# A hybrid four-layer kernel: the third layer's 16-token region gathered into one tile, and a forget gate whose scan adds two terms

## The chip, the cores and the metric

The kernel runs on one core of a Trainium2 chip. Its engines are TensorE (PE for products, PEld for the weight loads beside them), VectorE (DVE), ScalarE (ACT), GpSimd (POOL) and SyncE (SP), which issues the DMAs. Each engine works through its own queue in order and waits on semaphores for the others. The metric is the device time of one execution in microseconds, as the median of several runs. All of it runs in one launch.

## The reference

A meta prefix of 16 tokens and 1024 tokens of width 1024 pass four layers, each a residual branch behind an RMS norm: sliding-window attention, an mLSTM, an HGRN2 (the third layer, which the change touches), and attention again. The third layer has 8 heads with 128 key and 128 value channels:

```python
def hgrn2_chunkwise(q, k, v, log_f):
    ...
    def step(S, inp):
        q_, k_, v_, lf = inp
        A = jnp.cumsum(lf, axis=2)
        o_inter = jnp.einsum('bhtd,bhde->bhte', q_ * jnp.exp(A), S)
        dec = jnp.where(causal[..., None], A[:, :, :, None, :] - A[:, :, None, :, :], -jnp.inf)
        att = jnp.einsum('bhtd,bhtsd,bhsd->bhts', q_, jnp.exp(dec), k_)
        o = o_inter + jnp.einsum('bhts,bhse->bhte', att, v_)
        A_last = A[:, :, -1]
        S_new = jnp.exp(A_last)[..., None] * S + jnp.einsum('bhsd,bhse->bhde', k_ * jnp.exp(A_last[:, :, None] - A), v_)
        return S_new, o
...
    lb = lower_bound.astype(jnp.float32)
    lf = jnp.logaddexp(jnp.log(lb), jnp.log1p(-lb) + jax.nn.log_sigmoid(fpre.astype(jnp.float32)))
    kk = -jnp.expm1(lf)
```

The decay between two tokens differs by channel, so the attention matrix isn't one product: `exp(A_t - A_s)` has to be split at a point between s and t, and the kernel does that by levels of halves.

## The kernel before

Activations lie transposed: 128 channels on the partitions, the 1040 tokens along the row, in chunks of 400, 384 and 256. Each projection (`proj`, the products at L231) splits weight and activation into a high and a low part and sums three products. Weights arrive by DMA in halves of 128x512, which ACT casts and DVE subtracts (`split`, L195 and L196).

In the third layer (`layer_c`) every head has a forget gate `f_proj` (L1188 to L1202: log-sigmoid of z, the logaddexp with the lower bound, a scan by block of 128 tokens which gives A, and N, the log of the key less A), a query projection `q_proj` (L1211 is its last DVE step) and a mixer. The gate's `lna` and `lnb` are the logs of the two parts of the bound, `dif` is their difference, and each is a column of a tile named `lb` in the profile.

The mixer works on five regions: the first holds the 16 meta tokens, the other four two blocks of 128 tokens each. For a region, `level` builds a tile X for each of the levels 0 to 7 (levels 3 to 7 in the region of 16): two DVE steps fill the halves with exponents (L1247, L1248), ACT takes Exp (L1249), DVE multiplies the later half by Q (L1250). Level 7 is the diagonal (L1240, L1241). The X tiles rotate over 14 buffers. `levels_mm` then issues the products of all the levels in one burst (L1263 for levels 0 and 1, 32x64 and 32x32; L1273 for the others, 32x32, or 16x16 in the region of 16), into PSUM tiles `pm`. `tail0` masks and adds them on DVE (L1290, L1294, L1300), copies the attention tile together on POOL and ACT (`att`, L1302 to L1306), and prepares the decayed keys and queries (L1309, L1315). `tail1` transposes the keys on PE (`pt`, L1326), ACT copies them (`kT`, L1328), `states` multiplies them with the values (`pa`, L1336) and carries the state S on (L1341, L1343), and `tail2` makes the output (`po`, L1357, L1359).

What sets the order: PE's instructions stand as the program writes them. `weave(a, b)` merges two lists of steps so that both advance by the same share of their summed costs; steps of the list of a region carry a cost of GAP for each level and BURST for the products, and the tails carry lags (TAIL_LAG, KT_LAG, ATT_LAG) that only push the next step back. Each region's list is woven with the tail of the region ahead, and the whole with the projections of the next head, the gates and the output products, which fill PE between bursts. The order on the other engines comes from a scheduler at the build, which works with its own estimates and prefers steps wrapped in `hi`. All PSUM tiles share eight buffers.

## Time and profile before

| what | us |
| --- | --- |
| median of three runs | 2601.44 |
| lowest and highest | 2598.78, 2603.09 |
| profiled execution | 2596.91 |
| its span (first to last instruction) | 2595.1 |

In the rows of the profile, a timeline's row has the start in us from the span's begin, the duration of the merged instructions, engine, line, operation and tiles, and in brackets the idle time ahead of it with what ended it. A row of a group has, behind the bar, the busy time in us, the mean duration of one in ns, and the engine's idle time just ahead. A row of windows has the stretch, its length, the busy time of each engine and the granted TensorE clock. Matmuls are pipelined: their listed durations overlap, so the step from start to start is what one costs.

### The profile page before, as it was taken

The numbers are of one execution on the slowest core, as the hardware profiler recorded it, in microseconds if no ns is written. First come the engines' busy times: TensorE is split into PE (matmuls) and PEld (weight loads), VectorE is DVE, ScalarE is ACT, GpSimd is POOL, SyncE is SP. The second block draws the span as 40 slices with busy tenths as digits, with TensorE's granted clock in tenths as the row PEclk, the third lists the DMA queues.
The fourth block names the chain that finished last, engine by engine and source line by source line (L and its number), as shares of the span: only waits on it lengthen the run. The fifth ranks groups of instructions, "written<-read, shape, count | busy, mean of one in ns | idle before, by whom it ended". The sixth has DMA issues, their size and how long they took to land.

```text
span 2595.1 us, 54389 instructions
## 1 busy us (share of the span) xinstructions
PE 2547.2 (98%) x20446; PEld 2486.5 (96%) x20446; DVE 1960.2 (76%) x5290; ACT 1689.9 (65%) x4434; POOL 245.6 (9%) x564
## 2 busy tenths in 40 slices
PE   8999999999999999999999999999999999999999
PEld 8899999999999999999999999999999999999999
DVE  7897898775656564747474688988888978887996
ACT  8766766666464645555555757877676857767772
POOL 0321231000000000000000000010000000321330
PEclk9999999999999999999999999999999999999999
DMA  5223212021111111111111111111111113212112
GB/s 157 62 66 93 59 43 69 30 67 56 44 54 46 50 49 51 42 58 41 51 46 52 51 34 34 34 35 34 38 39 34 34 51 91 62 44 85 56 42 78
DMA packets 86058, 140.21 MB, mean 54 GB/s; under 512 B 12425, under 2 KB 39186, under 8 KB 85794
## 3 DMA queue, kind: packets, MB, share of 16 engines
q1 hardware_dynamic: 85794, 136.73, 17.1%
q8 instruction: 161, 2.64, 0.4%
q14 instruction: 103, 0.84, 0.1%
HBM read 121.83 MB, written 4.27 MB: 49 GB/s over the span
## 4 chain that ended last, share of the span: by engine, by line
PE 65%; DVE 13%; ACT 9%; issue 2%; DMA 2%; POOL 0%; SPq 0%; DVEq 0%; ACTq 0%; POOLq 0%
PE pj L231 29%; PE pj L326 15%; PE pj L281 10%; DVE wl L196 1%; ACT Sm L737 1%; PE po L1019 1%; PE po L1021 1%; PE pa L1035 1%; DVE Sm L734 1%; PE po L773 1%; ACT wh L195 1%; PE pt L755 1%; ACT X L1249 1%; PE pj L277 1%; DVE t L457 1%
## 5 line engine op out<-in xcount | busy, mean ns | idle before, releaser
L231 PE MATMUL pj<-uh,wh 128*128 128x256 f32 (+2 forms) x2688 | 914.8, 340 | 6.9 <-ACT uh L401 6.4
L231 PE MATMUL pj<-ul,wh 128*128 128x256 f32 (+2 forms) x2688 | 864.2, 322 | 0.3
L231 PE MATMUL pj<-uh,wl 128*128 128x256 f32 (+2 forms) x2688 | 864.3, 322 | 0.0
L231 PEld LDWEIGHTS pj<-uh,wh 128*128 128x128 f32 x2688 | 507.4, 189 | 16.3 <-ACT uh L401 6.4
L231 PEld LDWEIGHTS pj<-ul,wh 128*128 128x128 f32 x2688 | 507.9, 189 | 6.4 <-DVE ul L196 0.9
L231 PEld LDWEIGHTS pj<-uh,wl 128*128 128x128 f32 x2688 | 507.2, 189 | 0.0
L196 DVE TENSOR_TENSOR wl<-wr,wh 128x512 fp32r<-128x512 f32 (+1 forms) x338 | 234.7, 703 | 52.0 <-ACT wh L195 49.3
L195 ACT CAST wh<-wr 128x512 fp32r<-128x512 f32 (+1 forms) x338 | 202.9, 613 | 103.6 <-PE pj L326 32.7
L326 PE MATMUL pj<-yh,wh 128*128 128x384 f32 (+2 forms) x768 | 253.2, 330 | 9.8 <-DVE x L329 8.3
L329 DVE TENSOR_TENSOR x<-x,pj 128x384 f32<-128x384 f32 (+2 forms) x480 | 234.7, 509 | 32.8 <-PE pj L326 31.6
L326 PE MATMUL pj<-yl,wh 128*128 128x384 f32 (+2 forms) x768 | 245.8, 320 | 0.0
L326 PE MATMUL pj<-yh,wl 128*128 128x384 f32 (+2 forms) x768 | 245.8, 320 | 0.0
L281 PE MATMUL pj<-wh,uh 128*128 128x256 f32 (+1 forms) x768 | 232.7, 303 | 0.0
L281 PE MATMUL pj<-wl,uh 128*128 128x256 f32 (+1 forms) x768 | 216.4, 282 | 0.0
L281 PE MATMUL pj<-wh,ul 128*128 128x256 f32 (+1 forms) x768 | 215.9, 281 | 0.0
L737 ACT ACTIVATE Sm<-Sm,s 128x257 f32<-128x257 f32 (+2 forms) x272 | 131.1, 483 | 88.4 <-DVE s L734 85.9
L740 POOL TENSOR_TENSOR Sm<-Sm,s 128x512 f32<-128x512 f32 (+2 forms) x136 | 139.3, 1024 | 403.5 <-DVE s L739 383.3
L458 ACT ACTIVATE t<-t 128x384 f32<-128x384 f32 (+2 forms) x240 | 117.9, 491 | 76.5 <-DVE t L457 75.0
L326 PEld LDWEIGHTS pj<-yh,wh 128*128 128x128 f32 x768 | 144.5, 188 | 14.0 <-DVE x L329 10.4
L195 ACT CAST yh<-r 128x384 fp32r<-128x384 f32 (+2 forms) x120 | 57.0, 479 | 152.0 <-PE pj L326 136.3
L457 DVE SCALAR_TENSOR_TENSOR t<-pj,t 128x400 f32<-128x400 f32 (+2 forms) x168 | 86.5, 515 | 81.6 <-ACT t L456 80.3
L281 PEld LDWEIGHTS pj<-wh,uh 128*128 128x128 f32 x768 | 144.7, 188 | 2.2
(296 smaller groups left out, 5468.3 us busy)
## 6 DMA issues: line engine op xcount, KB each, us to landing
wr<-in_b_win SPq DMA_DIRECT2D x124, 256.0 KB, 2.8
wr<-in_a_win SPq DMA_DIRECT2D x80, 256.0 KB, 2.8
wr<-in_c_win SPq DMA_DIRECT2D x64, 256.0 KB, 2.8
wr<-in_a_wout SPq DMA_DIRECT2D x32, 256.0 KB, 3.0
wr<-in_b_wout SPq DMA_DIRECT2D x32, 256.0 KB, 2.7
t<-t SPq DMA_DIRECT2D x100, 48.0 KB, 1.9
cs<-in_rope SPq DMA_DIRECT2D x11, 400.0 KB, 3.6
cs<-in_rope SPq DMA_DIRECT2D x11, 384.0 KB, 3.5
```

The costliest lines, as they stand in the source:

```text
L195: s.copy(h, src)
L196: v.tensor_tensor(l, src, h.bitcast(F32), op=ALU.subtract)
L231: pe.matmul(acc[:, :cn], a[:, k, :], b[:, k, c0 : c0 + cn], start=(k == 0 and i == 0), stop=(k == KT - 1 and i == 2))
L277: pe.matmul(acc[:48, :nc], um[0][:, k, :], m[:, kk, :], start=(k == 0 and m is wh), stop=(k == KT - 1 and m is wl))
L281: pe.matmul(acc[:cn, :nc], a[:, k, c0 : c0 + cn], m[:, kk, :], start=(k == 0 and j == 0), stop=(k == KT - 1 and j == 2))
L326: pe.matmul(acc[:, :cn], a[:, k, mc], b, start=(k == 0 and i == 0), stop=(k == 1 and i == 2))
L329: v.tensor_tensor(x[:, m, c0 : c0 + cn], x[:, m, c0 : c0 + cn], acc[:, :cn], op=ALU.add)
L457: v.scalar_tensor_tensor(a[:, :cn], z, 0.0, a[:, :cn], op0=ALU.min, op1=ALU.subtract)
L458: s.activation(a[:, :cn], a[:, :cn], AF.Exp)
L734: v.tensor_tensor_reduce(Sm[:nq, u, :nk], S[:nq, u, :nk], R["masks"][:nq, P + mo : P + mo + nk], rq, sinks[u], ALU.add, ALU.min, st[:nq, u ...
L737: s.activation(Sm[:nq, u, : nk + 1], Sm[:nq, u, : nk + 1], AF.Exp, scale=-1.0, bias=st[:nq, u : u + 1], accum_out=den[:nq, u : u + 1])
L740: g.tensor_tensor(Sm[:nq, :, :nk], Sm[:nq, :, :nk], den[:nq].rearrange("p (u c) -> p u c", c=1).to_broadcast([nq, 2, nk]), op=ALU.mult)
```

## The change

Three things change in the third layer.

The forget gate. The logaddexp was built from `max(LS + dif, 0)`, then `+ lna + T1`; now it is `max(LS, -dif) + lnb` in one TENSOR_SCALAR, and the scan adds T1 itself: each step adds the element of `t1` and the element of `ls` to the running sum, where it multiplied by ones and added before. One SCALAR_TENSOR_TENSOR a chunk goes. At the layer's start, one ACT step makes `-dif`.

The region of 16 tokens. `first_levels` writes levels 3 to 7 into slices of one X tile and takes one Exp over its 80 columns. Its products no longer have a burst of their own; they are issued between the levels of region 1's burst, into a PSUM tile of their own, and its `tail0` follows that burst.

The order. Region 0 has no list to weave any more. The tail of the head before is woven with region 1; regions 0 and 1 have their tails one behind the other, woven with region 2; region 1's burst has a cost of 1.1 BURST.

```diff
-            R["lna"], R["lnb"], R["dif"] = lna, lnb, dif
+            s.mul(lna, dif, -1.0)
+            R["ndif"], R["lnb"], R["dif"] = lna, lnb, dif
...
-                v.tensor_scalar(LS, LS, dif, 0.0, op0=ALU.add, op1=ALU.max)
-                v.scalar_tensor_tensor(LS, LS, lna, T1, op0=ALU.add, op1=ALU.add)
+                v.tensor_scalar(LS, LS, ndif, lnb, op0=ALU.max, op1=ALU.add)
                 for b in CHUNK_BLOCKS[n]:
                     q0, nq = blk(b)
-                    v.tensor_tensor_scan(A[:, q0 : q0 + nq], ones[:, :nq], ls[:, q0 - c0 : q0 - c0 + nq],
-                                         0.0, ALU.mult, ALU.add)
+                    qs = slice(q0 - c0, q0 - c0 + nq)
+                    v.tensor_tensor_scan(A[:, q0 : q0 + nq], t1[:, qs], ls[:, qs], 0.0, ALU.add, ALU.add)
...
+            def first_levels():
+                A, NL, Q = (R[z, h][:, :16] for z in ("A", "N", "Q"))
+                X0 = xt()
+                X = {lv: X0[:, 16 * (lv - 3) : 16 * (lv - 2)] for lv in range(3, 8)}
+                for lv in range(3, 7):
+                    Av, Nv, Qv, Xv, mid = halves(lv, A, NL, Q, X[lv])
+                    v.tensor_tensor(Xv[:, :, 0, :], mid, Nv[:, :, 0, :], op=ALU.add)
+                    v.tensor_tensor(Xv[:, :, 1, :], Av[:, :, 1, :], mid, op=ALU.subtract)
+                v.tensor_tensor(X[7], A, NL, op=ALU.add)
+                s.activation(X0[:, :80], X0[:, :80], AF.Exp)
+                for lv in range(3, 7):
+                    Av, Nv, Qv, Xv, mid = halves(lv, A, NL, Q, X[lv])
+                    v.tensor_tensor(Xv[:, :, 1, :], Xv[:, :, 1, :], Qv[:, :, 1, :], op=ALU.mult)
+                for lv in X:
+                    W["X", 0, lv] = X[lv]
...
-            def levels_mm(r, lvs):
-                for lv in lvs:
+            def levels_mm(r):
+                for lv in range(8):
+                    if r == 1 and lv > 2:
+                        level_mm(0, lv)
                     level_mm(r, lv)
...
-                lvs = list(range(8)) if r else [3, 4, 5, 6, 7]
-                st = []
-                for lv in lvs:
+                st = [] if r else [S(0.0, first_levels)]
+                for lv in range(8 if r else 0):
                     st.append(S(0.0, level, r, lv))
                     st.append([GAP, lambda: None, None])
-                st.append(S(BURST if r else 0.2 * BURST, levels_mm, r, lvs))
-                st.append(S(0.0, tail0, r))
+                if r:
+                    st.append(S(BURST if r > 1 else 1.1 * BURST, levels_mm, r))
+                    st += [S(0.0, tail0, z) for z in ((0, 1) if r == 1 else (r,))]
                 main.append(st)
...
-            if h:
-                tails[0].append(held)
+            mx = main[0]
+            for r in range(1, 5):
+                mx += weave(main[r], last)
+                last = [[TAIL_LAG, lambda: None, None]]
+                if r == 1:
+                    last += ([held] if h else []) + tails[0]
+                last += tails[r]
             held = end
-            mx = []
-            for r in range(5):
-                mx += weave(main[r], last)
-                last = [[TAIL_LAG, lambda: None, None]] + tails[r]
             body += weave(mx, fill)
```

The rows below are the instructions as they stand in an engine's queue, with line, operation, tiles (with their numbers) and the shape written.

PE, head 0, the region of 16 tokens before: five products in a burst of their own, between projections (`pj`).

```order
L231 MATMUL pj_19320<-uh,wl_19096 128x256
L1273 MATMUL pm_19351<-X_19315 16x16
L1273 MATMUL pm_19351<-X_19327 16x16
L1273 MATMUL pm_19351<-X_19332 16x16
L1273 MATMUL pm_19351<-X_19337 16x16
L1273 MATMUL pm_19351<-Q_19275,X_19348 16x16
L231 MATMUL pj_19320<-uh,wh_19095 128x256
```

PE, head 0, the same products now, in region 1's burst (L1293 is L1273 moved down), the 16x16 ones between the 32x32 ones.

```order
L1293 MATMUL pm_19394<-X_19345 32x32 x8
L1293 MATMUL pm_19403<-X_19313 16x16
L1293 MATMUL pm_19394<-X_19350 32x32 x8
L1293 MATMUL pm_19403<-X_19313 16x16
L1293 MATMUL pm_19394<-X_19361 32x32 x8
L1293 MATMUL pm_19403<-X_19313 16x16
L1293 MATMUL pm_19394<-X_19366 32x32 x8
L1293 MATMUL pm_19403<-X_19313 16x16
L1293 MATMUL pm_19394<-X_19371 32x32 x8
L1293 MATMUL pm_19403<-Q_19273,X_19313 16x16
L1293 MATMUL pm_19394<-Q_19273,X_19382 32x32 x8
```

The burst now begins six 256-wide products behind the place where the lone one stood, and region 0's transposition, state and output products come behind it.

DVE, head 0, region 3, before: from the two multiplies behind the gate's TENSOR_SCALAR for the second chunk to the last multiply by Q that the burst needs (the last row). The rows of L1200 are the scans.

```order
L1250 TENSOR_TENSOR X_19814<-X_19814,Q_19275 128x32x4
L1250 TENSOR_TENSOR X_19819<-X_19819,Q_19275 128x64x2
L1197 SCALAR_TENSOR_TENSOR t_19702<-t_19702,lb_18765,t_19701 128x384
L1247 TENSOR_TENSOR X_19830<-r_18841,N_18842 128x128
L1200 SCALAR_TENSOR_TENSOR r_19515<-ones,t_19702 128x128 x3
L1240 TENSOR_TENSOR X_19842<-r_18841,N_18842 128x256
L1202 SCALAR_TENSOR_TENSOR r_19516<-r_19516,lb_18766,r_19515 128x384
L1248 TENSOR_TENSOR X_19830<-r_18841 128x128
L1343 SCALAR_TENSOR_TENSOR S_19838<-S_19632,s_19750,pa_19835 128x128
L1191 SCALAR_TENSOR_TENSOR t_19778<-pj_19717,t_19777 128x256
L1343 SCALAR_TENSOR_TENSOR S_19840<-S_19838,s_19750,pa_19835 128x128
L1250 TENSOR_TENSOR X_19830<-X_19830,Q_19275 128x128
```

DVE, the same place now: the gate's TENSOR_SCALAR (L1197), the last two multiplies (L1270, with X_19811 the last that the burst needs), and the scans (L1201) behind them.

```order
L1193 TENSOR_TENSOR r_19552<-t_19691,pj_19582 128x384
L1322 TENSOR_REDUCE rd_19719<-t_19716 128x64
L1197 TENSOR_SCALAR t_19691<-t_19691,lb_18765,lb_18766 128x384
L1270 TENSOR_TENSOR X_19806<-X_19806,Q_19273 128x64x2
L1270 TENSOR_TENSOR X_19811<-X_19811,Q_19273 128x128
L1332 TENSOR_TENSOR X_19930<-X_19930,Q_19273 128x256
L1201 SCALAR_TENSOR_TENSOR r_19551<-t_19690,t_19691 128x128 x3
```

The last multiply moved from behind the gate's scans and the next chunk's first step to ahead of the scans.

ACT, head 0, the copy of region 0's transposed keys (`kT` of 16x128, the last row of each piece) before:

```order
L454 ACTIVATE t_19308<-pj_19283 128x384
L455 ACTIVATE t_19308<-t_19308 128x384
L456 ACTIVATE t_19308<-t_19308,consts 128x384
L1309 ACTIVATE X_19549<-r_18841 128x256
L1315 ACTIVATE X_19552<-N_18842,r_18841 128x128 x2
L458 ACTIVATE t_19308<-t_19308 128x384
L195 CAST wh_19969<-wr_19971 128x512
L1328 COPY kT_19406<-pt_19405 16x128
```

ACT, the same copy now, with region 1's attention copies (L1326, L1328), region 2's Exps (L1269) and two weight casts ahead of it:

```order
L1326 COPY att_18794<-pm_19385 64x2x64
L1328 COPY att_18794<-pm_19385 32x2x32 x2
L1269 ACTIVATE X_19531<-X_19531 128x256
L1269 ACTIVATE X_19526<-X_19526 128x256
L1269 ACTIVATE X_19540<-X_19540 128x256
L454 ACTIVATE t_19455<-pj_19333 128x256
L195 CAST wh_19956<-wr_19958 128x512
L455 ACTIVATE t_19455<-t_19455 128x256
L195 CAST wh_19956<-wr_19962 128x512
L456 ACTIVATE t_19455<-t_19455,consts 128x256
L1269 ACTIVATE X_19569<-X_19569 128x256
L1350 COPY kT_19516<-pt_19515 16x128
```

The copy moved behind region 1's burst and part of region 2's levels; on PE, six projection products now stand between its transposition and the state product, where there were twelve of them, region 1's burst and six more.

More of the change, by code (lines that the diff above doesn't have):

```diff
@@ L1183, in evac @@
                 cs = slice(c0, c0 + cn)
-                lna, lnb, dif = (R[key][:, h : h + 1] for key in ("lna", "lnb", "dif"))
+                ndif, lnb, dif = (R[key][:, h : h + 1] for key in ("ndif", "lnb", "dif"))
                 z = acc[:, :cn]
@@ L1232, in xt, with halves @@
                 return R["mix"].tile([P, 256], F32, tag="X", name=nm("X"), bufs=XS)
+            def halves(lv, A, NL, Q, X):
+                hh = 64 >> lv
+                view = lambda t: t.rearrange("p (g two h) -> p g two h", two=2, h=hh)
+                Av, Nv, Qv, Xv = view(A), view(NL), view(Q), view(X)
+                mid = Av[:, :, 0, hh - 1 : hh].to_broadcast(list(Av[:, :, 0, :].shape))
+                return Av, Nv, Qv, Xv, mid
+            def first_levels():
[13 more added lines that the diff above has]
+                    W["X", 0, lv] = X[lv]
             def level(r, lv):
@@ L1242, in level @@
                     return
-                hh = 64 >> lv
-                view = lambda t: t.rearrange("p (g two h) -> p g two h", two=2, h=hh)
-                Av, Nv, Qv, Xv = view(A), view(NL), view(Q), view(X[:, :cn])
-                mid = Av[:, :, 0, hh - 1 : hh].to_broadcast(list(Av[:, :, 0, :].shape))
+                Av, Nv, Qv, Xv, mid = halves(lv, A, NL, Q, X[:, :cn])
                 v.tensor_tensor(Xv[:, :, 0, :], mid, Nv[:, :, 0, :], op=ALU.add)
@@ L1265, in level_mm @@
                     return
-                if "pf" not in W:
-                    W["pf"] = psum("pm", 2)
-                pf = W["pf"][:, :384].rearrange("p (b l t) -> p b l t", b=2, l=6)
+                if ("pf", r) not in W:
+                    W["pf", r] = psum("pm", 2)
+                pf = W["pf", r][:, :384].rearrange("p (b l t) -> p b l t", b=2, l=6)
                 w = 32 if r else 16
@@ L1284, in tail0 @@
                 A, NL, Q = R["A", h][:, cs], R["N", h][:, cs], R["Q", h][:, cs]
-                pf = W.pop("pf")[:, :384].rearrange("p (b l t) -> p b l t", b=2, l=6)
+                pf = W.pop(("pf", r))[:, :384].rearrange("p (b l t) -> p b l t", b=2, l=6)
                 nb, w, f0 = len(REGIONS[r]), (32 if r else 16), (0 if r else 1)
```

## The prediction

> **What bounds the kernel now.** I read the page first, then the busy times of the stretch in which the third layer's mixer runs, then PE's waits in it, and then the timelines around those waits.
>
> ```profile
> span 2595.1 us, 54389 instructions
> ...
> PE 2547.2 (98%) x20446; PEld 2486.5 (96%) x20446; DVE 1960.2 (76%) x5290; ACT 1689.9 (65%) x4434; POOL 245.6 (9%) x564
> ```
>
> TensorE is the bound: it idles 48 us of 2595. Work taken from DVE or ACT is worth something only where PE waits for it. The third layer's mixer runs from 1560 to 2100 us, and its row (span, then busy us of PE, PEld, DVE, ACT and POOL, then the granted clock) is:
>
> ```profile
> 1560.00:2100.00 540.00, 531.12 (x6930) 512.59 (x6930) 461.44 (x1509) 408.76 (x1163) 46.65 (x145) 0.99 0.12 38
> ```
>
> So 8.9 us of PE idle time lie where the change is, DVE is at 85% there and ACT at 76%. PE's waits in that stretch, in total, times and longest:
>
> ```profile
> PE pa L1336 <- ACT kT L1328: 5.3, 6, 1.9
> PE pm L1273 <- DVE X L1250: 2.1, 1, 2.1
> PE po L1357 <- POOL att L1302: 1.2, 2, 1.0
> ```
>
> That is 8.6 of the 8.9 us. One wait is for a level (the multiply by Q), six for the copy of the transposed keys, two for the attention tile. The level wait is in head 0, region 3, and it costs more than its length, since the projections behind it run slower:
>
> ```profile
> 1618.83 0.75 PE L1273 MATMUL pm<-X 128*32 128x32 f32 x61
> 1621.68 0.33 PE L1273 MATMUL pm<-X 128*32 128x32 f32 x16 [2.10 <-DVE X L1250]
> ...
> 1622.53 0.34 PE L231 MATMUL pj<-uh,wl 128*128 128x400 f32 x1
> 1622.71 0.46 PE L231 MATMUL pj<-uh,wh 128*128 128x400 f32 x1
> ...
> 1625.30 0.54 PE L231 MATMUL pj<-uh,wl 128*128 128x400 f32 x1
> 1625.63 0.63 PE L1357 MATMUL po<-att,v 128*128 128x128 f32 x2
> ```
>
> ```profile
> 1622.00:1626.00 4.00, 4.00 (x32) 3.96 (x19) 3.76 (x15) 2.47 (x10) 0.00 (x0) 0.60 0.02 4
> 2093.00:2097.00 4.00, 3.96 (x15) 3.96 (x16) 2.87 (x7) 2.45 (x5) 0.59 (x1) 0.60 0.44 131
> 2025.40:2029.40 4.00, 3.98 (x126) 3.73 (x127) 3.95 (x18) 3.65 (x14) 1.00 (x4) 1.00 0.00 0
> ```
>
> The granted clock is 0.60 in the 4 us behind this wait, and 0.60 behind the last layer-end wait of 1.91 us at 2093.04. Behind the wait of 1.71 us at 2025.42 it stays 1.00. From 1622.71 to 1625.63 nine 400-wide products took 2.92 us; at their usual step of 0.18 (1622.53 to 1622.71) they would take 1.62, so the slow clock cost 1.3 us.
>
> The Trainium skill (TensorE: Matmul & The Clock Gate, Part 1: The HAM clock gate) says that the clock falls after an idle window of about 3.4 us. By that the wait of 2.10 us would cost nothing beyond itself, and my sum would be 1.3 us smaller. The trace differs, with 0.60 granted behind 2.10 us, and decides.
>
> **The change, part by part.**
>
> *The lone bursts of region 0.* Today each of eight heads has a small burst of its own for the 16 tokens:
>
> ```profile
> 1646.39 0.34 PE L231 MATMUL pj<-uh,wl 128*128 128x384 f32 x1
> 1646.66 0.36 PE L1273 MATMUL pm<-X 128*16 128x16 f32 x8
> 1646.87 0.20 PE L1273 MATMUL pm<-Q,X 128*16 128x16 f32 x2
> 1647.00 0.91 PE L1373 MATMUL pa<-t,ones 128*128 128x384 f32 x2
> ...
> L1273 PE MATMUL pm<-X 128*32 128x32 f32 x2560 | 31.2, 200 | 2.1 <-DVE X L1250 2.1
> ```
>
> From the last projection's start (1646.39) to the next wide product (1647.00) pass 0.61 us where 0.18 is the step, so 0.43. In head 0 the same is 1595.46 to 1596.22, 0.76 where 0.12 is the step:
>
> ```profile
> 1595.46 0.28 PE L231 MATMUL pj<-uh,wl 128*128 128x256 f32 x1
> 1595.77 0.47 PE L1273 MATMUL pm<-X 128*16 128x16 f32 x8
> ...
> 1596.22 0.39 PE L231 MATMUL pj<-uh,wh 128*128 128x256 f32 x1
> 1596.45 0.28 PE L231 MATMUL pj<-ul,wh 128*128 128x256 f32 x1
> ```
>
> That is 0.64, and the step behind it (1596.45 less 1596.22) is 0.11 too long as well. With that after-effect the two are 0.54 and 0.75; I take 0.55, since head 0 runs while its inputs are just ready: 8 x 0.55 = 4.4 us go. The ten rows come back in region 1's burst. At the mean of the 32-wide rows (31.2 us for 2560, 12 ns) the 80 rows cost 1.0 us; at the step of the lone burst's rows (0.21 us for eight, 26 ns) 2.1. They all go to the first partitions, as the lone ones do, but other groups can run beside them; between the two I take 18 ns, 1.4 us. Term: **-3.0** (from -3.4 to -2.3).
>
> *The level wait of head 0, region 3.* DVE's queue explains it:
>
> ```profile
> 1616.97 0.41 DVE L1196 TENSOR_SCALAR t<-t,lb 128x384 f32<-128x384 f32 x1
> 1617.30 0.48 DVE L1250 TENSOR_TENSOR X<-X,Q 128x128 f32<-128x128 f32 x2
> 1617.70 0.61 DVE L1197 SCALAR_TENSOR_TENSOR t<-t,lb,t 128x384 f32<-128x384 f32 x1
> ...
> 1618.48 1.04 DVE L1200 TENSOR_TENSOR_SCAN r<-ones,t 128x128 f32<-128x128 f32 x3
> ...
> 1621.34 0.28 DVE L1250 TENSOR_TENSOR X<-X,Q 128x128 f32<-128x128 f32 x1
> ```
>
> The last multiply stood behind the removed instruction (L1197), three scans and seven others (the order is shown with the change). In the changed order it stands directly behind the TENSOR_SCALAR, with one other multiply ahead of it, so it would end about 1617.4 + 2 x 0.2 + 0.1 = 1617.9, and PE needs it at 1619.6 (0.75 us after 1618.83). The wait goes unless the queue runs 1.7 us later, and its slow clock with it: -2.1 - 1.3 = **-3.4** (bounds -3.4 and 0).
>
> *Head 0's merged burst.* It stands six 256-wide products behind the place of the lone one, so at about 1595.46 + 7 x 0.12 = 1596.3. The multiplies cannot start before Q is there:
>
> ```profile
> 1595.55 1.81 DVE L1250 TENSOR_TENSOR X<-X,Q 128x8 f32<-128x8 f32 x11
> ```
>
> These eleven (region 0's four and region 1's seven) end at 1597.36 in either order, and the burst wants the last near its end, 0.7 us on. So a new wait of **+0.4** (0 to 1.1).
>
> *The key copies.* Region 0's transposition and state product now follow region 1's burst and share one stretch with region 1's. PE's work between transposition and state product covers the copy on ACT. By the order and the steps above it falls in head 0 from 1597.74 to 1602.73 to six products, 6 x 0.18 = 1.1 us, and there the copy stands behind region 2's Exps and two weight casts:
>
> ```profile
> 1597.74 0.27 PE L1326 MATMUL pt<-ident,X 128*16 128x128 f32 x1
> 1602.73 0.38 PE L1336 MATMUL pa<-v,kT 128*128 128x128 f32 x2
> ...
> 1598.80 0.25 ACT L1328 COPY kT<-pt 16x128 f32<-16x128 f32 x1
> ...
> L195 ACT CAST wh<-wr 128x512 fp32r<-128x512 f32 x70 | 42.4, 613 | 13.9 <-DMA wr<-in_c_win 9.6 <-PE pj L326 1.9 <-DMA wr<-in_c_wout 1.8
> ```
>
> In the other heads it is some 2.2 to 2.7 us. A copy takes 0.4 us but has landed up to 4.3 us after its transposition, as at 2088.57, whose product started at 2093.04. If each of eight copies were 0.2 late, +1.6; if head 0's were 1.1 and four others 0.6 late, +3.5. Against that, region 4's cover grows by some 1 us in the heads 0 to 5, and at 2025.42 (1.71) the copy stands ahead of the two weight casts of 0.61 that it followed, which takes off some 1.2. The end wait at 2093.04 (1.91) keeps its casts ahead of it and stays. Term: **0** (from -3.4, all but the end's, to +3.5).
>
> *The attention tile* waits 1.2 us in all for DVE's reduction and POOL's copies, whose order around it barely moves: **0** (-1.2 to +1.0, one more wait like the longest).
>
> *DVE and ACT.* 24 instructions L1197 go, and 32 of the 40 small Exps become none:
>
> ```profile
> L1197 DVE SCALAR_TENSOR_TENSOR t<-t,lb,t 128x400 f32<-128x400 f32 x8 | 5.1, 633 | 4.4 <-ACT t L1195 4.4
> L1197 DVE SCALAR_TENSOR_TENSOR t<-t,lb,t 128x384 f32<-128x384 f32 x8 | 4.9, 612 | 0.0
> L1197 DVE SCALAR_TENSOR_TENSOR t<-t,lb,t 128x256 f32<-128x256 f32 x8 | 3.8, 479 | 0.9 <-ACT t L1195 0.8
> L1249 ACT ACTIVATE X<-X 128x16 f32<-128x16 f32 x32 | 6.3, 210 | 1.6 <-DVE X L1248 1.5
> ```
>
> That is 13.8 us of DVE and, with wider Exps in their place, some 5 of ACT, all beside PE's work: no term of its own. Without that cover it could give no more than the waits counted above. The scan reads a second tile instead of the ones, of the same size and type; were it slower, it would be by no more than L1197 gave back. One negation of eight columns at the layer's start is hidden under the first projections.
>
> **Sum.** -3.0 - 3.4 + 0.4 + 0 + 0 = -6.0 us. The profiled execution took 2596.9 us, of which 2595.1 are span; the median of three is 2601.4, 4.5 above it. From the median: **2595.4**, 0.23% less. About 0.2%, 5.2 us, is what can be told from no change, so "faster" begins at 2596.2.
>
> **Rivals.**
>
> *The gain goes into key copies.* PE comes sooner to region 0's products, and ACT isn't relieved as much as PE. Against it: ACT has some 5 us less to do. With the upper ends of the two zero terms, -6.0 + 3.5 + 1.0 = -1.5: 2599.9.
>
> *Alternating widths cost PE.* The merged burst changes ten times a head between 16 and 32 columns, which the trace of before never shows. Entering a small burst costs 0.1 us (1646.39 to 1646.66 is 0.27 where 0.18 is the step); at that for each change 80 x 0.1 = 8 us: +2.0, 2603.4. The Trainium skill (TensorEngine Tiling (Array Packing), Key Properties) says that a change of tiling mode drains TensorE, which speaks for this, though its list of modes has none narrower than 32 columns.
>
> *Slower: PSUM.* All products share eight buffers, and three of them now fill in one burst instead of two. They are read late: the burst that begins at 2012.71 is read at 2022.98.
>
> ```profile
> 2012.71 0.47 PE L1263 MATMUL pm<-X 128*32 128x64 f32 x13
> ...
> 2022.98 0.61 DVE L1290 TENSOR_TENSOR t<-pm,masks 128x192 f32<-128x192 f32 x2
> ```
>
> Were PE to meet an unread buffer in every head and wait 2 us, 8 x 2 - 6 = +10: 2611. It decides from 0.75 us a head. Against it: PE waits for no buffer in this layer now, and the count of buffers used is the same.
>
> *All waits go* except the end's: the key copies at -3.4, the attention tile at -1.2, no new wait: -3.0 - 3.4 - 3.4 - 1.2 = -11.0, 2590.4; with the end's wait and its slow clock 2587.
>
> **How the numbers follow.** The forecast has 0.52 (its own range 2592 to 2599; 0.36 of it faster, 0.16 the same), all waits going 0.13 (faster), the key copies 0.18 (0.16 the same, 0.02 slower), the widths 0.09 (0.06 the same, 0.03 slower), PSUM 0.08 (slower). Faster 0.49, same 0.38, slower 0.13. The range 2588.5 to 2604 leaves out PSUM and the tail of the gain.
>
> **What would show it.** Eight groups of 16-wide products gone from their own places, and PE's busy time in the mixer some 3 us less; no wait for L1250's successor in head 0, region 3, and a clock of 1.00 there; waits for the key copy still near 5 us in total, some of them now in region 0. I am wrong if the merged burst takes over 0.4 us longer than the others, if waits for key copies pass 9 us, or if PE waits for the mask products.

## The result, and the profile after

The changed kernel takes 2592.88 us (median of 7 runs, 2587.62 to 2594.76), the kernel before beside it 2598.92 (7 runs): a ratio of 0.9974, 95% interval 0.9964 to 0.9984, so 6.0 us less. In a second comparison the two were 2592.82 (11 runs) and 2597.52 (30 runs): 0.9983, 0.9974 to 0.9991, or 4.7 us. The forecast was 6.0 us less: 2595.4 us, with a range from 2588.5 to 2604. It was counted from 2601.4; here the kernel before was itself 2.5 us faster.

From the page of the changed kernel, the span and the engines:

```profile
span 2593.0 us, 54342 instructions
...
PE 2547.2 (98%) x20446; PEld 2487.2 (96%) x20446; DVE 1949.5 (75%) x5266; ACT 1682.9 (65%) x4403; POOL 243.4 (9%) x564
```

DVE has 10.7 us less to do and ACT 7.0. TensorE's busy time is the same to 0.1 us, but the two aren't alike: its instructions take longer while its clock is slow, and this execution lost 8.5 us of full clock ahead of 2500 us, the one before 3.4. The third layer's mixer, in the same window as before (span, busy us of PE, PEld, DVE, ACT, POOL, clock), and all that TensorE waits for in it:

```profile
1560.00:2100.00 540.00, 532.73 (x6986) 514.26 (x6986) 456.19 (x1500) 409.90 (x1152) 44.22 (x145) 1.00 0.12 38
```

```profile
PE pa L1358 <- ACT kT L1350: 7.0, 7, 1.6
```

In these rows L1293 is the L1273 of before, L1358 is L1336, L1350 is L1328, L1270 and L1253 are L1250; in the programs below they shift by one to three.

TensorE idles 7.3 us where it idled 8.9. The waits for a level and for the attention tile are gone; what is left is waits for the key copy, 7.0 us for 5.3.

This profiled execution took 2594.76 us, only 2.2 below the one before, although the layer gained more. A cut at two waits that stand at the same products in every program of the table below shows where. TensorE's timeline at the two, first of the kernel before, then of the changed one:

```profile
1546.97 0.39 PE L326 MATMUL pj<-yh,wh 128*128 128x256 f32 x1 [1.44 <-DVE x L329]
...
2150.32 0.39 PE L326 MATMUL pj<-yh,wh 128*128 128x256 f32 x1 [1.44 <-DVE x L329]
```

```profile
1549.41 0.39 PE L326 MATMUL pj<-yh,wh 128*128 128x256 f32 x1 [1.44 <-DVE x L329]
...
2144.84 0.39 PE L326 MATMUL pj<-yh,wh 128*128 128x256 f32 x1 [1.44 <-DVE x L329]
```

Between them lie 603.35 us before and 595.43 after: 7.9 less. Ahead of the first cut, in code that didn't change, the changed kernel's execution lost 2.4 us, and behind the second 3.4. Those are spells of slow clock, told of in the last section: two ahead of the cut cost 1.6 and 1.4 us, with 0.5 gained elsewhere, and one behind it the 3.4. They fall in one execution and not in another.

The stretch is the measure used below. It splits into three parts: TensorE's idle time in the mixer (540 less the busy time in the window above), the time lost to the slow clock (over windows of 5 us with less than 0.97 granted, 5 times what is missing to 1), and the rest, which is work. Before: 603.4 = 8.9 + 3.4 + 591.1. Changed: 595.4 = 7.3 + 0 + 588.2. So of the 7.9 us, 2.9 are work, 1.6 waits and 3.4 slow clock.

### The profile page after: what moved, and what is told of

Same layout as the page of the kernel before. It is cut to its first block, busy times and chain, and to the rows that moved or that the text cites. A ratio compares the mean times of both kernels' runs of the same rounds, so it can differ in the third digit from the quotient of the medians.

```text
span 2593.0 us, 54342 instructions
## 1 busy us (share of the span) xinstructions
PE 2547.2 (98%) x20446; PEld 2487.2 (96%) x20446; DVE 1949.5 (75%) x5266; ACT 1682.9 (65%) x4403; POOL 243.4 (9%) x564
## 4 chain that ended last, share of the span: by engine, by line
PE 62%; DVE 13%; ACT 8%; issue 2%; DMA 1%; SPq 0%; POOL 0%; DVEq 0%; ACTq 0%; POOLq 0%
PE pj L231 28%; PE pj L326 14%; PE pj L281 10%; DVE wl L196 1%; PE po L1019 1%; PE po L1021 1%; PE pa L1035 1%; ACT X L1269 1%; PE po L773 1%; DVE x L329 1%; PE pj L277 1%; ACT Sm L737 1%; PE pt L755 1%; DVE Sm L734 1%; DVE X L1267 1%
```

## The experiments

All ratios are to the kernel before on the same chip, with 95% intervals. The last four columns are from one profile each, in us.

| program | ratio | interval | stretch | idle | slow clock | rest |
| --- | --- | --- | --- | --- | --- | --- |
| before | 1 | | 603.4 | 8.9 | 3.4 | 591.1 |
| changed | 0.9974 | 0.9964 to 0.9984 | 595.4 | 7.3 | 0 | 588.2 |
| changed, again | 0.9983 | 0.9974 to 0.9991 | 595.9 | 7.8 | 0 | 588.2 |
| forget gate alone | 0.9986 | 0.9977 to 0.9995 | 599.9 | 7.7 | 1.7 | 590.5 |
| one tile alone | 0.9982 | 0.9971 to 0.9993 | 596.7 | 5.3 | 0 | 591.4 |
| gate and tile, own burst | 0.9992 | 0.9983 to 1.0001 | 598.2 | 6.8 | 0 | 591.4 |
| tile and merged burst, gate of before | 0.9990 | 0.9980 to 1.0000 | 599.3 | 8.7 | 1.7 | 588.9 |
| changed, products grouped | 0.9975 | 0.9964 to 0.9986 | 596.6 | 7.4 | 0 | 589.3 |
| before, KT_LAG 1500 | 0.9989 | 0.9980 to 0.9998 | 597.2 | 5.2 | 1.7 | 590.2 |
| changed, KT_LAG 1500 | 0.9966 | 0.9955 to 0.9978 | 592.9 | 4.8 | 0 | 588.1 |
| the same, norm's sum later | 0.9977 | 0.9967 to 0.9987 | 593.8 | 5.9 | 0 | 587.9 |
| changed, DVE copies region 0's keys | 1.0009 | 1.0001 to 1.0018 | 603.2 | 13.4 | 1.7 | 588.1 |
| both: KT_LAG 1500 and DVE copies | 0.9979 | 0.9971 to 0.9988 | 594.1 | 6.6 | 0 | 587.5 |

My theory throughout: TensorE is the bound, so only its own work and its waits count; the merged burst takes some 3 us of work away, the level wait goes, and the waits that are left are key copies with too little work between the transposition and the product.

**The forget gate alone.** On the kernel before:

```diff
-                v.tensor_scalar(LS, LS, dif, 0.0, op0=ALU.add, op1=ALU.max)
-                v.scalar_tensor_tensor(LS, LS, lna, T1, op0=ALU.add, op1=ALU.add)
+                v.tensor_scalar(LS, LS, ndif, lnb, op0=ALU.max, op1=ALU.add)
...
+                    v.tensor_tensor_scan(A[:, q0 : q0 + nq], t1[:, qs], ls[:, qs], 0.0, ALU.add, ALU.add)
```

> The kernel before with only the forget gate's part of the change. TensorE's order is the one of before, so the lone bursts stay. My theory (TensorE is the bound, and DVE's time pays only where TensorE waits for DVE): the level wait of head 0, region 3 shrinks from 2.10 us to some 0.4 to 0.9 us, because one instruction of 0.61 us and part of the queue ahead of the last multiply go, but the three scans still stand there; waits for key copies stay near 5.3 us; the time falls by 1.5 us (0 to 3). Rival (DVE is at 85% in the mixer and its 13.8 us, of which 24 instructions go, count in the time): 6 us or more, the whole gain of the change.

2595.01 us against 2597.88, 2.9 less; neither 1.5 nor 6 can be excluded by the interval. TensorE's waits in the mixer:

```profile
PE pa L1336 <- ACT kT L1328: 5.6, 6, 2.4
PE po L1357 <- POOL att L1302: 1.2, 2, 1.0
PE pm L1273 <- DVE X L1250: 0.9, 1, 0.9
```

The level wait is 0.9, as expected, the others stay, and the spell of slow clock behind it is gone. I had left that spell out of this expectation: 1.2 of wait and 1.7 of clock make up most of the stretch's 3.4. DVE's work counts where TensorE waits for DVE, and the other instructions of L1197 are worth little: the rest column falls by 0.6.

**One tile alone.** On the kernel before, levels 3 to 7 of the 16-token region in one X tile with one Exp (`first_levels`), their products in their own burst, TensorE's order as before:

```diff
-                lvs = list(range(8)) if r else [3, 4, 5, 6, 7]
-                st = []
-                for lv in lvs:
+                st = [] if r else [S(0.0, first_levels)]
+                for lv in range(8 if r else 0):
                     st.append(S(0.0, level, r, lv))
                     st.append([GAP, lambda: None, None])
```

> The kernel before, with the one part of the change that puts the 16-token region's levels into one tile with one Exp; its products keep their own burst, TensorE's order is the one of before, and the forget gate is the one of before. My theory (ACT's 5 us lie beside TensorE's work): no term, the waits for kT stay at 5.3 us within 1, the level wait at 2.1, and the time is the same as before within 1.5 us. Rival (32 Exps fewer let ACT be sooner with the copies): the waits for kT fall by 2 us or more, and the time by as much.

2593.72 against 2599.07: 5.4 less (4.7 by the ratio), which contradicts "no term". The waits fall, but not mainly those for copies:

```profile
PE pa L1356 <- ACT kT L1348: 4.4, 5, 1.2
PE po L1379 <- DVE S L1363: 0.3, 1, 0.3
PE po L1377 <- POOL att L1322: 0.2, 1, 0.2
```

The level wait is 0.11 us, too short for this list, and the 1.2 us for the attention tile became 0.2. In head 0 a wait of 1.17 for a copy now stands just ahead of the burst, where 0.38 was; it gives DVE the time, so that 2.48 us of waiting in two places became 1.28 in nearly one, and the clock stays at 1.00. So the level wait goes with this part alone, and shrinks to 0.9 with the gate alone. Neither needs the other, and their gains don't add up.

**Both, with the own burst.** The changed kernel, its moved products put back:

```diff
-                for lv in range(8):
-                    if r == 1 and lv > 2:
-                        level_mm(0, lv)
+                for lv in range(8) if r else range(3, 8):
                     level_mm(r, lv)
```

> The changed kernel without the part that moves products: forget gate and one-tile levels as changed, but the 16-token region's products in a burst of their own again, and its tail where it stood before. My theory (what the merged burst takes off TensorE, some 3 us, it gives back as waits for region 0's key copies, which now have less work in front of them): TensorE's lone bursts are back, the waits of region 0 (4.4 us) are gone, no level wait over 0.3 us, TensorE idles 3.5 to 5 us in the mixer, and the time is the changed kernel's within 1.5 us. Rival (the merged burst carries the gain): 3 us or more above the changed kernel. A third way (the two parts on DVE and ACT carry all of it): 3 us or more below the changed kernel.

2596.30 against 2598.13, 0.9992 (0.9983 to 1.0001): in ratio 0.0009 to 0.0018 above the changed kernel's two results, 2 to 5 us, beyond the 1.5 of my theory and nearer to the rival, though the intervals overlap. The profile has both halves of the theory:

```profile
PE pa L1356 <- ACT kT L1348: 5.2, 6, 1.6
PE po L1377 <- POOL att L1322: 1.3, 2, 1.1
```

The waits of region 0 are gone, but those for the attention tile are back and regions 2 and 3 of head 0 wait 1.00 and 1.62. TensorE idles 0.5 less than in the changed kernel and works 3.2 more. By these numbers the merged burst is worth its work with the new gate.

**Tile and merged burst, with the gate of before.** The changed kernel with the diff of the forget gate undone:

```diff
+                v.tensor_scalar(LS, LS, dif, 0.0, op0=ALU.add, op1=ALU.max)
+                v.scalar_tensor_tensor(LS, LS, lna, T1, op0=ALU.add, op1=ALU.add)
-                v.tensor_scalar(LS, LS, ndif, lnb, op0=ALU.max, op1=ALU.add)
```

> The changed kernel with the forget gate of before (24 SCALAR_TENSOR_TENSOR more on DVE). My theory: the lone bursts are gone (3 to 4 us of TensorE time), the level wait of head 0, region 3 is gone, since the last multiply now stands ahead of the scans, and the key copies wait about 7 us as in the changed kernel; the time is within 1.5 us of the changed kernel's, some 5 to 6 us below before. Rival (the gain needs what the gate takes off DVE): 2 us or less below before, with a new wait for a level or for Q.

2595.53 against 2597.88: 2.4 less (0 to 5.2), nearer to the rival. The level wait is gone and the work is down, both as expected, but:

```profile
PE pa L1358 <- ACT kT L1350: 7.4, 7, 2.2
PE po L1379 <- DVE att L1316: 0.7, 1, 0.7
PE pm L1293 <- DVE X L1270: 0.4, 2, 0.2
```

Three short waits for DVE stand there, and the wait at the layer's end is 2.16 with a spell of slow clock behind it. Against the program with one tile alone, merging takes 2.5 us of work off and adds 3.4 of idle time and 1.7 of slow clock. So with the gate of before, where DVE has more to do, the merged burst gains nothing that these profiles show. That DVE's load is the reason is likely and not shown: one spell makes up 1.7 of it, and the ratios of the two programs overlap.

**The width that changes ten times.** The changed kernel with the 16-wide products together, ahead of region 1's:

```diff
-                for lv in range(8):
-                    if r == 1 and lv > 2:
+                if r == 1:
+                    for lv in range(3, 8):
                         level_mm(0, lv)
+                for lv in range(8):
                     level_mm(r, lv)
```

> The changed kernel, but the products of the 16-token region stand together ahead of region 1's in the burst, so that the width changes twice a head and not ten times. My theory (the alternating widths cost TensorE little): the burst takes as long as in the changed kernel within 0.15 us a head, and the time is the same within 1.5 us. Rival (each change of width costs 0.1 us): the burst is 0.8 us shorter a head, and the time some 6 us below the changed kernel's. A third way: the small products run beside the large ones only where they alternate, and together they take up to 0.3 us more a head, 2 us above the changed kernel.

0.9975 (0.9964 to 0.9986), the same as the changed kernel. The burst in head 3 (starts in us), first changed, then the changed kernel's next burst without 16-wide products, then grouped:

```profile
1769.85 0.50 PE L1283 MATMUL pm<-X 128*32 128x64 f32 x15
...
1771.08 0.36 PE L1293 MATMUL pm<-Q,X 128*16 128x16 f32 x18
1771.37 0.44 PE L231 MATMUL pj<-uh,wh 128*128 128x384 f32 x1
```

```profile
1803.16 0.50 PE L1283 MATMUL pm<-X 128*32 128x64 f32 x15
...
1804.55 0.38 PE L281 MATMUL pj<-wh,uh 128*128 128x256 f32 x1
```

```profile
1767.43 0.37 PE L1293 MATMUL pm<-X 128*16 128x16 f32 x8
...
1769.06 0.45 PE L231 MATMUL pj<-uh,wh 128*128 128x384 f32 x1
```

1.52, 1.39 and 1.63 us. Ten products of 16 columns cost 0.13 us between the wide ones and 0.24 ahead of them, so alternating is the cheaper way, by 0.11 us a head; the rest column has 1.1 us for eight. The other heads agree: the merged burst takes 1.50 or 1.51 us in all eight of the changed kernel, its 24 bursts without 16-wide products 1.38 on average (1.31 to 1.47), and the grouped one 1.62 (1.58 to 1.69). That is within the 0.15 us of my theory, on the side of the third way; the rival, by which grouping would gain 0.8 us a head, is out.

**More work in front of the copy.** The changed kernel, and then the kernel before, with

```diff
-KT_LAG, ATT_LAG = 900.0, 600.0
+KT_LAG, ATT_LAG = 1500.0, 600.0
```

> The changed kernel with KT_LAG 1500 for 900: more projections stand between the transposition of the keys and the product that reads the copy, in every region (in region 0 some 2.2 to 4.0 us of TensorE work for 1.2 to 2.7). My theory (the waits that are left are key copies which the work between doesn't cover): TensorE's waits for kT fall from 7.0 us to 3 us or less, those of region 0 to 1 us or less, and the time is some 4 us below the changed kernel's, 10 below before. Rival (ACT is late anyway, and who is pushed back meets the next thing late): the waits move to the attention tile, to the level tiles or to the next region's copy, TensorE's idle time in the mixer stays above 6 us, and the time is within 1.5 us of the changed kernel's.

> The kernel before with KT_LAG 1500 and nothing else. My theory (waits for kT are a matter of the work between, with or without the change): the 5.3 us of waits for kT fall to 1.5 or less, except that the one at the layer's end, whose copy stands behind casts that wait for a DMA, keeps some 0.5; the level wait of 2.1 us and the lone bursts stay; the time is 3 to 4 us below before. Rival (the longer distance pays only once region 0's copies are in the way): the time is the same as before within 1 us.

Changed: 2589.60 against 2597.88, 8.3 less (5.7 to 11.7). Before: 2592.76 against 2597.52, 4.8 less by the medians, though the ratio of 0.9989 (0.9980 to 0.9998) is 2.9. TensorE's waits, first of the changed kernel with the longer lag, then of the kernel before with it:

```profile
PE pa L1395 <- ACT t L1389: 3.2, 3, 1.6
PE po L1381 <- DVE S L1365: 0.6, 1, 0.6
PE pa L1358 <- ACT kT L1350: 0.6, 1, 0.6
```

```profile
PE pa L1336 <- ACT kT L1328: 2.2, 2, 1.4
PE pm L1273 <- DVE X L1250: 1.7, 1, 1.7
PE po L1357 <- POOL att L1302: 1.2, 2, 1.0
```

Waits for copies fall from 7.0 to 0.6 and from 5.3 to 2.2, so they are a matter of the work between, with the change or without. But 3.2 us come back at the norm's sum, which waits for the squares that ACT makes; idle time falls by 2.4, not by 6.4. This is the fastest program of the study, and it beats both kernels in its stretch, by 2.5 us against the changed one; its ratio's interval overlaps that of the changed kernel.

**The norm's sum later.** The same program, with

```diff
-                    last += ([held] if h else []) + tails[0]
+                    last += tails[0] + ([held] if h else [])
```

> The kernel of the run with KT_LAG 1500, in which also the norm's sum for the last chunk of the head before (`held`, whose product of the ones L1395 waited 3.2 us in all for ACT's squares) stands behind region 0's tail instead of ahead of it. My theory (what a step's cover is, in TensorE work between producer and consumer, decides each of the waits that are left): the waits of L1395 for ACT fall from 3.2 us to under 0.5, those for kT stay under 1 us, TensorE idles some 2 us in the mixer instead of 4.8, and the time is some 2 us below that run, 10 below before. Rival (ACT's queue is what is late, and each wait that goes comes back at the next step): idle time in the mixer stays at 4.5 us or more, and the time is the same within 1 us.

0.9977 (0.9967 to 0.9987): no gain, and the theory falls here. The waits for the sum are gone, as meant, and the copies wait again:

```profile
PE pa L1358 <- ACT kT L1350: 4.0, 4, 1.5
```

Idle time is 5.9 us for 4.8, as the rival has it. The reading that fits: a wait that TensorE no longer has is time that ACT no longer gets, and the next step meets ACT as late as before, since at a head's begin ACT is nearly full. From 1640 to 1660 us, in the run with the longer lag alone:

```profile
1640.00:1660.00 20.00, 18.43 (x228) 17.52 (x227) 18.07 (x57) 18.62 (x53) 2.38 (x8) 1.00 0.11 34
```

ACT is busy 18.62 and DVE 18.07 of 20 us, TensorE 18.43. Over the mixer ACT's share is 76%, but here it limits as much as TensorE.

**Another engine for the copy.** The changed kernel with region 0's keys copied by DVE, and the same with KT_LAG 1500:

```diff
-                s.copy(kT[:bn, :w], pt[:bn, :w])
+                if r == 0:
+                    v.tensor_copy(kT[:bn, :w], pt[:bn, :w])
+                else:
+                    s.copy(kT[:bn, :w], pt[:bn, :w])
```

> The changed kernel, in which DVE and not ACT copies region 0's transposed keys (eight copies of 16x128, one a head); everything on TensorE stands as it is. In the changed kernel these copies landed 0.6 to 3.2 us after their transposition, with 1.2 to 2.7 us of TensorE work between, and the waits of region 0 were 4.4 of 7.0 us. My theory (the copy is late because ACT's queue stands full of casts and Exps where the head begins): the waits of region 0 fall under 1.5 us, those for kT in all to 4 us or less, and the time is some 2.5 us below the changed kernel's. Rival (whichever engine copies is late: DVE is at 84% in the mixer, and by the queue's order the copy stands behind three products with the masks): the waits of region 0 stay at 3 us or more and the time is the same within 1 us, or later, where what DVE is kept from is a level.

> The changed kernel with both: KT_LAG 1500 and region 0's keys copied by DVE. My theory: the waits for kT are under 1 us as with KT_LAG 1500 alone, and ACT, which has one copy less where the head begins, is sooner with the squares that L1395 waits for (3.2 us there); TensorE idles 3.5 us in the mixer instead of 4.8, and the time is 9 to 11 us below before. Rival (what limits the head's begin is the sum of ACT's work there, of which 0.25 us is nothing): idle time stays at 4.5 us or more and the time is that of KT_LAG 1500 alone within 1 us.

Without the longer lag 2599.60 against 2599.07, so the whole gain is lost. TensorE's waits up to 2095 us (the one at the layer's end, for ACT's copy, adds 1.97):

```profile
PE pa L1361 <- DVE kT L1351: 9.4, 5, 3.5
PE pa L1361 <- ACT kT L1353: 1.9, 4, 1.0
```

DVE's queue ahead of the worst of them, in head 1 (TensorE's transposition started at 1654.72, its product at 1660.63):

```profile
1655.66 1.05 DVE L1201 TENSOR_TENSOR_SCAN r<-t,t 128x128 f32<-128x128 f32 x3
...
1657.29 0.68 DVE L196 TENSOR_TENSOR wl<-wr,wh 128x512 fp32r<-128x512 f32 x1
...
1659.82 0.46 DVE L1400 SCALAR_TENSOR_TENSOR r<-r,ogain,t 128x256 f32<-128x256 f32 x1
1660.21 0.27 DVE L1351 COPY kT<-pt 16x128 f32<-16x128 f32 x1
```

The copy of 0.27 us stands behind three scans, a subtraction of weights, the products with the masks, the reductions and a norm's multiply. DVE is the worse of the two. With the longer lag the time is 2593.23, 0.9979, no better than the lag alone, and my theory falls there too: region 0's copies are still waited for in heads 0 and 1 (0.85 and 1.84 us), the norm's sum waits 2.5 for 3.2, and TensorE idles 6.6 us for 4.8.

**Seven PSUM buffers.** The changed kernel with one buffer less:

```diff
-        return ps.tile([P, 512], F32, tag="p", name=nm(tag), bufs=8)
+        return ps.tile([P, 512], F32, tag="p", name=nm(tag), bufs=7)
```

> The changed kernel with seven shared PSUM buffers for eight. It tests the rival by which three PSUM tiles that fill in one burst make TensorE wait for an unread one. My theory (there is room): no wait of TensorE for a product tile to be read, or under 1 us in the third layer, and a time within 2 us of the changed kernel's; the other layers share the buffers too and can add waits of their own, which the stretch of the third layer leaves out. Rival (eight buffers are just enough): waits of some 2 us in every head, 16 us or more above the changed kernel's time in the third layer alone.

2596.01 us, 0.9990 (0.9981 to 0.9999), some 2 to 4 us above the changed kernel. TensorE idles some 2 us more than there between 1540 and 2160 us and 2.7 more in the other layers; the stretch is 599.3, of which 8.2 are idle time, 1.7 slow clock and 589.4 the rest. In the mixer one wait is new:

```profile
PE pm L1293 <- ACT att L1328: 0.9, 1, 0.9
```

It is 0.9 us for a buffer to be read, with seven; with eight, as the list of the changed kernel shows, there is none. The rival of the buffers is out.

**The changed kernel again.**

> The changed kernel once more, beside the three others on the same chip, with a profile of its own. My theory (the spells of slow clock fall by chance behind waits of 1.6 us and more, in code that is the same): the waits for kT stand at the same places within 0.3 us, 7 us in all; the spells of slow clock stand behind other waits than in the first profile, and none stands where no wait of 0.4 us or more is ahead; the time is 0.1% to 0.35% below before. Rival (the spells belong to places of the program): the same seven windows of 5 us are slow, those at 345 and 2170 us too.

Eight of the ten waits of the mixer (of 0.09 us and more) stand at the same products within 0.15 us. Two differ: one of 0.11 us became 1.03, and the one at the layer's end 0.96 for 1.24; they are 7.6 us in all by the list of waits. The stretch is 595.9 for 595.4. The spells of slow clock are behind waits near 243 and 404 us, where the first profile had them near 68, 344, 403 and 2169: one of four is in both. The rival falls, and the spells don't belong to places of the program.

## Why the prediction was right, and where it was not

**Lone bursts, -3.0: right.** The rest column is 590.2 to 591.4 in the five programs with the lone bursts and 587.5 to 588.9 in the seven of the table with the alternating one; the means differ by 2.8. (The program with seven PSUM buffers has 589.4, of which 0.5 is more waiting ahead of the second cut.) Of my two ends for the ten rows that come back, the lower is true: 0.13 us a head, 1.0 in all for my 1.4.

**Level wait of head 0, region 3, -3.4: right in size, 2.1 of wait and 1.7 of clock.** The order was as I read it: the last multiply stands directly behind the TENSOR_SCALAR. DVE's queue in the changed kernel:

```profile
1619.35 0.48 DVE L1197 TENSOR_SCALAR t<-t,lb,lb 128x384 f32<-128x384 f32 x1
1619.73 0.54 DVE L1270 TENSOR_TENSOR X<-X,Q 128x128 f32<-128x128 f32 x2
...
1620.57 1.08 DVE L1201 TENSOR_TENSOR_SCAN r<-t,t 128x128 f32<-128x128 f32 x3
```

It ends at 1620.27, 2.4 us later than I had worked out. That is about what both whole programs are apart at the layer's begin (1549.41 and 1546.97), so against the cut it is where I put it.

**Head 0's merged burst, +0.4: wrong, no wait.** The burst stands at 1598.82, 1596.4 against the cut, as forecast; but the last multiplies on which it waits end at about 1599.5, and the products that read them come late enough in a burst that lasts 1.5 us. It was inside its bounds.

**Key copies, 0 (-3.4 to +3.5): the step that was off, by +1.9.** They went from 5.35 to 7.27 us. Region 0's four waits (heads 0, 1, 3 and 5: 1.57, 1.15, 0.62, 1.06) are the 4.4 new us, and the others fell by 2.5. In head 0 it went as the prediction's own row-reading had it: TensorE's transposition and product,

```profile
1603.31 0.27 PE L1348 MATMUL pt<-ident,X 128*16 128x128 f32 x1
...
1606.24 0.46 PE L1358 MATMUL pa<-v,kT 128*128 128x128 f32 x2 [1.57 <-ACT kT L1350]
```

with six products between, and on ACT two casts of weights, parts of Q and an Exp ahead of the copy:

```profile
1603.64 0.61 ACT L195 CAST wh<-wr 128x512 fp32r<-128x512 f32 x1
...
1604.47 0.60 ACT L195 CAST wh<-wr 128x512 fp32r<-128x512 f32 x1
1604.98 0.51 ACT L456 ACTIVATE t<-t,consts 128x256 f32<-128x256 f32 x1
1605.54 0.42 ACT L1269 ACTIVATE X<-X 128x256 f32<-128x256 f32 x1
1605.86 0.24 ACT L1350 COPY kT<-pt 16x128 f32<-16x128 f32 x1
```

The prediction set gains in other regions against this loss and took the sum as 0. They came, above all where it had named one (the wait of 1.71 at 2025.42 is gone) and at the layer's end (1.24 for 1.91), but the loss of 4.4 is nearly double them, and more than the +3.5 that I had put as its worst. The work between was read rightly: 1.4 us in head 0 and 2.2 to 2.8 in the others. What I had too small is how late the copy is: it ended 0.9 to 3.5 us after the start of its transposition, where before it was 0.6 to 1.9.

**Attention tile, 0 (-1.2 to +1.0): at its lower end.** All three waits (1.34 us, one of them too short for the list) are gone in both profiles of the changed kernel. With the own burst they are there still, with the new gate (1.2 and 1.3) as with the longer lag (1.2), but not with one tile alone (0.2). So the gate by itself doesn't end them, and they can shrink without the merged burst; the runs don't show which step it is.

**The end's wait "stays": half right.** It stayed, at 1.24 and 0.96 us for 1.91, and without the slow clock. Its copy stands behind two casts of weights, which wait for their DMA: over the 14 profiles it is 0.6 to 2.4 us. That is another 1.7 us which I had not counted, and by the last section such a spell depends on where in time the wait happens to fall.

**DVE and ACT, no term: wrong as a rule, though it did no harm to the sum.** Either part alone gains 3 to 5 us. The level wait and the clock behind it are 2.9 us of the gate's 3.4 in the stretch, and 3.7 of the tile's 6.7. In the sum of all parts that is the -3.4, counted once.

So the terms came to -2.9 of work, -2.1 for the level, -1.3 for the attention tile, +1.9 for copies and -3.4 of slow clock, -7.8 to the stretch's -7.9, where I had -6.0. Runs give -6.0 and -4.7. The two terms that I set to zero were off in opposite directions, so that the sum came out as it did is in part luck; the two terms that make it up, the bursts and the level wait, are not. The rivals: some of the gain did go into copies, 1.9 us; alternating costs nothing against grouping; no buffer is waited for; and not all waits went.

What stays open: what each part is worth to a microsecond. The parts' ratios have intervals of some 5 us, and their waits of 1 to 2 us come and go from one order of the queues to another.

## What to carry to other kernels

When an engine is 98% busy, sum two things only, its own work and its waits, and read each wait from the queue of the engine that is late: a part that "only" relieves another engine is worth the waits that it ends, once, whichever part comes first. A wait that is pushed out by more distance can come back at the next step if the late engine is full there: look at its share in the 20 us around the wait, not in the layer. Cut the trace at two events that both programs share before reading a difference of 0.2%, and count up to 1 us more for a wait of 2 us, for what it does to the clock.

## What the runs showed of the hardware that was not expected

**Whether the clock falls behind a wait depends on the wait's length and on where in time it falls.** The same wait for the same tile, in the first layer, with nothing changed there: TensorE's timeline and the windows' row for the 4 us from 68 us on (the clock is the third number from the end), first of the kernel before, then of the changed one:

```profile
67.85 0.39 PE L755 MATMUL pt<-ident,Sm 128*16 128x128 f32 x2 [2.17 <-POOL Sm L740]
```

```profile
68.00:72.00 4.00, 3.64 (x30) 3.27 (x28) 3.16 (x8) 2.21 (x6) 2.14 (x3) 1.00 0.68 218
```

```profile
67.76 0.39 PE L755 MATMUL pt<-ident,Sm 128*16 128x128 f32 x2 [2.17 <-POOL Sm L740]
```

```profile
68.00:72.00 4.00, 4.00 (x24) 3.73 (x22) 3.07 (x7) 2.29 (x6) 2.14 (x3) 0.58 0.70 204
```

Over the 14 profiles, counting TensorE's waits of 0.3 us and more ahead of 2500 us (but not the first, of 6 to 7 us for the first input), and the windows of 4 us with a clock under 0.95 behind them: 33 of 59 waits of 2 us and more were followed by a spell, 8 of 59 from 1.5 to 2 us, none of 81 from 1 to 1.5, and 1 of 219 shorter ones. The 42 spells took 75.7 us of full clock, 1.8 each. An execution lost 1.7 to 10.2 us of full clock in this way, about as much as the runs of one kernel differ (2587.62 to 2594.76 for the changed one). That the spells make that spread is likely and not shown, since only one execution of each is profiled. By these counts I estimate that a wait of 2 us costs 33/59 x 1.8, another 1.0 us on average, and one under 1.5 next to nothing. It is an upper figure, since lost clock isn't always lost time: behind the spell at 68 us the next product that waits stands at 75.77, and in the kernel before, without a spell, at 75.96.

What looks like chance is mostly the place of the wait on a grid. Each spell has a clock of 0.50 for 3.41 us (three for twice that), and within an execution all spells begin a whole number of times 3.41 us apart. Cut by that grid, the kernel before was busy for 1.57 us of the window from 66.31 to 69.72, across whose start the wait of 2.17 fell, and no spell followed; the changed kernel was busy for 1.24 us of the window from 65.22 to 68.63, which held the whole wait, and one followed at 68.63. Over all profiles a spell followed each of the 33 windows in which TensorE idled more than 1.9 us, 7 of the 102 with 1.2 to 1.9, and 2 of the others. Why those nine fell and others didn't stays open.

The Trainium skill (TensorE: Matmul & The Clock Gate, Part 1: The HAM clock gate) puts the fall of the clock behind an idle window of about 3.4 us, and calls the window free-running. The grid of 3.41 us agrees with the second; the first doesn't hold here if it means a window without work, since little more than 1.9 us of idle time in a window were enough. The longest of these waits, 3.49 us in the program in which DVE copies, was split between two windows, of which TensorE idled 1.89 and 1.60 us, and no spell followed (its row, and the windows' row behind it):

```profile
1660.63 0.46 PE L1361 MATMUL pa<-v,kT 128*128 128x128 f32 x2 [3.49 <-DVE kT L1351]
```

```profile
1664.00:1668.00 4.00, 4.00 (x132) 3.72 (x132) 3.54 (x15) 3.65 (x12) 0.00 (x0) 1.00 0.03 6
```

**Narrow products ride along.** Ten products of 16 columns cost 0.13 us between 32-wide ones, 0.24 in front of them, and 0.43 to 0.5 in a burst of their own (by the prediction's row at 1646.39, and by the rest column: 2.8 / 8 + 0.13). That is what the merged burst is worth: 2.4 to 2.9 us in eight heads.
